# Moving the low halves of the weights to GpSimd and the high masks to VectorE in the attention of a hybrid decoder block

## Chip, cores and metric

The kernel runs on one core of one Trainium2 chip. The metric is the device time of one execution in microseconds; lower is better. A core has five engines that run their own instruction streams and wait for each other through semaphores: TensorE (PE in the profile; its weight loads stand apart as PEld), VectorE (DVE), ScalarE (ACT), GpSimd (POOL) and SyncE (SP, which here issues the DMAs).

## The reference

A decoder block over 512 tokens of width 2048, all in float32. After an RMS norm, one large projection feeds two branches: sliding-window attention (32 query heads, 4 key/value heads of width 64, window 128, a sink per head) and a gated delta rule (16 key heads, 32 value heads). Each branch is projected back, the two are merged by sigmoid gates, projected and added to the input, and a last norm follows. The attention, to which the change belongs, for each block of 128 queries and the 256 keys that it can see:

```python
s = jnp.einsum('bqhgd,bkhd->bhgqk', q_blk, k_blk).astype(jnp.float32) * scale
s = jnp.where((band & kv_ok[None, :])[None, None, None], s, -jnp.inf)
m = jnp.maximum(jnp.max(s, axis=-1, keepdims=True), sink)
p = jnp.exp(s - m)
p = p / (jnp.sum(p, axis=-1, keepdims=True) + jnp.exp(sink - m))
return jnp.einsum('bhgqk,bkhd->bqhgd', p.astype(v_blk.dtype), v_blk)
```

## The kernel before

**Precision by halves.** Every large product is made from three products of a shorter float format (fp32r): a value is split into a high half (`whi`, a cast by ACT) and a low half (`wlo`, the value minus its high half), and high x high, high x low and low x high are summed. For weights, `split` (L161) does this: one cast of 128x1024 (L162) and two subtractions of 128x512 (L165). The subtractions go to the engine that stands in `lo_eng[0]` at that time. Weight tiles come by DMA in half-tiles of 8 x 128 rows; `w32`, `whi` and `wlo` have three buffers each, so the cast for a half-tile waits until TensorE has done the high products of the third half-tile before it, and the subtractions until it has done that half-tile's low products.

**A projection** (`proj`, L183) is two half-tiles. `mm_half` (L171) does 16 matmuls with the high weights (L174, L176) and then 8 with the low weights (L179). After each matmul it calls `flow.tick()`.

**Order.** TensorE's instructions keep the order in which the program writes them. Other work is written as generators in `Flow`: each says after how many ticks it wants to go on, and its TensorE instructions are thereby placed between those of the projections. The order on DVE, ACT, POOL and SP is not written out; the framework that builds the program sorts each engine's instructions by when it reckons them ready and by their place in the program. At run time each engine takes its queue strictly in that order.

**Stages.** (1) norm and transposes, 0 to about 70 us; (2) key and query convolutions and their inverse matrices, to about 810; (3) the delta rule, to 1815, with `lo_eng[0] = pool` (L632); (4) the attention, 1815 to 2205, with `lo_eng[0] = dve` (L663); (5) the branch projections and merge, to 2726; (6) the output projection and last norm.

**The attention.** Four groups `g` of eight heads. While the projections of queries and of some gates run, `scores(g, b, ...)` (L703) handles the query block `b` = 0 to 3 in two halves of four heads (`i2`): per half, TensorE makes scores of four heads into two PSUM banks, `pa` and then `pb` (L717, L718); DVE adds the mask and takes the maximum (L722, it reads the bank) and folds the two key blocks into one by another maximum (L725; the window of 128 makes a key of the block before and one of this block exclude each other in every column); ACT takes the exponential and its sums (L733); DVE adds the sink's part (L734) and takes the reciprocal (L735); POOL normalizes (L736).

`weighted(g, b, scs)` (L747) follows some ticks later: per half, TensorE transposes the probabilities (L757), ACT casts them to the high half `pth` (L759) and DVE makes the low half `ptl` (L760). Both have an unmasked copy (index 0, for the block's own keys) and, if `b` is not 0, a masked one (index 1, for the difference to the block before): POOL masks the high half (L763), DVE the low half (L764), two instructions of 128x256 each per half. Then TensorE multiplies with the values (L774, into the banks `pc` and `tr`), ACT and DVE add the two parts (L776, L777), POOL multiplies with the gate (L778), and a DMA stores the result. `pth` and `ptl` have one buffer each.

Of the kernel before, what the change touches and what calls it, by code (L numbers as in the profile page):

```python
# [8 lines left out]
F32 = mybir.dt.float32  # L9
# [3 lines left out]
ALU = mybir.AluOpType  # L13
# [66 lines left out]
def hybrid_block(  # L80
# [21 lines left out]
    pe, dve, act, pool = nc.tensor, nc.vector, nc.scalar, nc.gpsimd  # L102
# [10 lines left out]
    def new_pool(stack, name, bufs, side="left"):  # L113
        return stack.enter_context(tc.tile_pool(name=name, bufs=bufs, side=side, reuse_waits="tile"))
# [4 lines left out]
    def bank(tag, bufs=1):  # L119
        return ps.tile([P, S], F32, name=tag, bufs=bufs)  # L120
# [31 lines left out]
    lo_eng = [dve]  # L152
# [507 lines left out]
                flow.drain()  # L660


    lo_eng[0] = dve  # L663
    actx = ctx.enter_context(ExitStack())
    pa = new_pool(actx, "pa_", 2)
    amask = pa.tile([P, 3 * P], F32, name="amask", bufs=1)
# [36 lines left out]
    def scores(g, b, qt, kd):  # L703
# [36 lines left out]
        def go():  # L740
            values_.add(weighted(g, b, scs))
            yield 0
# [4 lines left out]
    def weighted(g, b, scs):  # L747
        zs = pa.tile([P, 4, P], F32, name="za")
        nc.sync.dma_start(zs, za_d[4 * g:4 * g + 4, :, b * P:(b + 1) * P].rearrange("t p n -> p t n"))
        pth = pa.tile([P, 2, 2, 4, P], F32R, name="pth", bufs=1)  # L750
        ptl = pa.tile([P, 2, 2, 4, P], F32R, name="ptl", bufs=1)
        mb = before.unsqueeze(1).unsqueeze(1).broadcast_to([P, 2, 2, P])
        for i2, sc in enumerate(scs):
            tp = bank("tr", 2).rearrange("p (a j n) -> p a j n", a=2, j=2)
            for par in range(2):
                for j in range(2):
                    pe.transpose(tp[:, par, j, :], sc[:, 2 * j + par, :], ident)  # L757
            ph, pl = (pp[:, :, :, 2 * i2:2 * i2 + 2, :] for pp in (pth, ptl))
            act.copy(ph[:, :, 0], tp)  # L759
            dve.tensor_tensor(pl[:, :, 0], tp, ph[:, :, 0].bitcast(F32), ALU.subtract)  # L760
            if b:
                for a in range(2):
                    pool.tensor_tensor(ph[:, a, 1], ph[:, a, 0].bitcast(F32), mb[:, a], ALU.mult)  # L763
                    dve.tensor_tensor(pl[:, a, 1], pl[:, a, 0].bitcast(F32), mb[:, a], ALU.mult)  # L764
            yield 8
        done_b[0] += 1
        yield 4
        t = pa.tile([P, S], F32, name="at", bufs=1)
        oz = pa.tile([P, S], F32, name="gt").rearrange("p (i n) -> p i n", i=4)
        for par, r, r2 in ((0, H0, H1), (1, H1, H0)):  # L770
            op = bank("tr", 2) if par else bank("pc")
            todo = [(kind, n, pp) for kind in range(2 if b else 1) for n, pp in ((par, pth), (2 + par, ptl))]
            for i, (kind, n, pp) in enumerate(todo):
                pe.matmul(op, vpad[g % 2][kind][:, b - kind, n:n + 2, :].rearrange("p c d -> p (c d)"),  # L774
                          pp[:, par, kind].rearrange("p i n -> p (i n)"), start=i == 0, stop=i == len(todo) - 1)
            act.copy(t[r], op[r2])  # L776
            dve.tensor_tensor(t[r], t[r], op[r], ALU.add)  # L777
        pool.tensor_tensor(oz, t.rearrange("p (i n) -> p i n", i=4), zs, ALU.mult)  # L778
        nc.sync.dma_start(od_d[4 * g:4 * g + 4, :, b * P:(b + 1) * P].rearrange("t p n -> p t n"), oz)
        yield 6  # L780
# [39 lines left out]
    actx.close()  # L820


    op_ = new_pool(ctx, "op", 8)

    def branch(q, pl):
# [168 lines left out]
```

## Time and profile before

| | |
|---|---|
| median of 3 runs (range) | 2913.93 us (2913.84 to 2914.82) |
| the profiled execution: time, span | 2914.18 us, 2912.4 us |
| granted TensorE clock, mean | 0.997 |
| DMA moved, share of 16 engines by the large queue | 376.07 MB, 40.7% |
| attention, 1815 to 2205 us: ACT busy | 195.46 us |

The span is the time from the first to the last instruction in the trace; the time of the execution has a little more around it. A row of a group of instructions reads: line of the kernel, engine, operation, output<-inputs by the program's names, shape, count | busy time in us, mean duration of one in ns | idle time of the engine just before them and what ended it. A row of the timeline reads: start in us, duration in us, engine, line, operation, names, shape, count [idle time before it, and what ended it]; with a count over 1 the duration is that of several in a row. A row of waits reads: who waited for whom: total us, times, longest. A row of a stretch (A:B) has its length and then for each engine the busy us and the number of instructions (PE, PEld, DVE, ACT, POOL), the granted clock, the DMA share and GB/s. In the view of one line, a row has the shortest, median and longest duration in ns.

### The profile page before, as it was taken

What the parts mean: (1) busy time and instruction counts of PE and PEld (TensorE: products, weight loads), DVE (VectorE), ACT (ScalarE), POOL (GpSimd) and SP (SyncE); (2) the same over time, 40 slices, a digit from 0 to 9 for tenths busy, and PEclk for the clock granted to TensorE, in tenths of its full rate; (3) what the DMA queues carried; (4) which work ended last, traced back from release to release, by engine and by line L of the source; (5) the groups of instructions that cost most, each with busy time, mean ns of one, the idle gap of its engine ahead of it and who ended that gap; (6) DMA issues with size and microseconds to landing.
All of it is one profiled execution on the core that took longest, in us unless ns stands there. A gap on an engine that the chain in (4) does not pass through costs nothing.

```text
span 2912.4 us, 36773 instructions
## 1 busy us (share of the span) xinstructions
PE 2850.0 (98%) x13594; PEld 2370.9 (81%) x13594; DVE 1762.9 (61%) x3520; ACT 1028.6 (35%) x1645; POOL 555.8 (19%) x464
## 2 busy tenths in 40 slices
PE   7999999999999999999999999999999999999998
PEld 7778888888888888888878888877788888888887
DVE  6686667979825555555555554478884455455434
ACT  5532222232333343334333333355553222122222
POOL 2310000000033334333334333024230000000010
PEclk9999999999999999999999999999999999999999
DMA  3344444353553333333333322424237555554533
GB/s 132 115 123 142 135 136 151 125 207 116 174 153 100 103 110 103 105 98 116 98 109 109 104 89 94 133 87 113 91 109 225 172 174 163 156 163 147 181 100 103
DMA packets 184628, 376.07 MB, mean 129 GB/s; under 512 B 65505, under 2 KB 82273, under 8 KB 183041
## 3 DMA queue, kind: packets, MB, share of 16 engines
q1 hardware_dynamic: 184448, 373.72, 40.7%
q8 instruction: 108, 1.77, 0.3%
q14 instruction: 72, 0.58, 0.1%
HBM read 316.97 MB, written 54.59 MB: 128 GB/s over the span
## 4 chain that ended last, share of the span: by engine, by line
PE 88%; DVE 8%; ACT 2%; issue 1%; POOL 0%; DMA 0%; SPq 0%; ACTq 0%; DVEq 0%
PE acc L179 24%; PE acc L176 24%; PE acc L174 24%; PE pa L555 2%; PE pb L574 2%; PE fo L902 1%; PE fo L900 1%; PE fo L901 1%; PE acc L247 1%; PE tr L529 1%; DVE ptl L764 1%; DVE o L616 1%; DVE ro L197 1%; DVE wlo L165 1%; DVE ad L381 1%
## 5 line engine op out<-in xcount | busy, mean ns | idle before, releaser
L174 PE MATMUL acc<-hT_hi,whi 128*128 128x512 f32 x2592 | 1038.5, 401 | 0.0
L176 PE MATMUL acc<-hT_lo,whi 128*128 128x512 f32 x2592 | 1018.7, 393 | 0.0
L162 ACT CAST whi<-w 128x1024 fp32r<-128x1024 f32 x446 | 467.7, 1049 | 1166.5 <-PE acc L176 940.4
L179 PE MATMUL acc<-hT_hi,wlo 128*128 128x512 f32 x2592 | 685.1, 398 | 2.2 <-DVE wlo L165 2.2
L165 POOL TENSOR_TENSOR wlo<-w,whi 128x512 fp32r<-128x512 f32 x284 | 363.3, 1300 | 1231.8 <-PE acc L179 643.7
L165 DVE TENSOR_TENSOR wlo<-w,whi 128x512 fp32r<-128x512 f32 x608 | 424.0, 720 | 261.1 <-ACT whi L162 204.5
L176 PEld LDWEIGHTS acc<-hT_lo,whi 128*128 128x128 f32 x2592 | 488.6, 188 | 92.8
L174 PEld LDWEIGHTS acc<-hT_hi,whi 128*128 128x128 f32 x2592 | 488.3, 188 | 92.9
L179 PEld LDWEIGHTS acc<-hT_hi,wlo 128*128 128x128 f32 x2592 | 479.6, 188 | 98.1 <-DVE wlo L165 3.1
L176 PE MATMUL acc<-dl,whi 128*128 128x512 f32 x768 | 298.8, 389 | 0.0
L174 PE MATMUL acc<-dh,whi 128*128 128x512 f32 x768 | 298.8, 389 | 0.0
L179 PE MATMUL acc<-dh,wlo 128*128 128x512 f32 x768 | 189.7, 389 | 0.0
L297 DVE SCALAR_TENSOR_TENSOR cy<-acc,cw,cy 128x511 f32<-128x511 f32 (+2 forms) x192 | 142.8, 744 | 62.9 <-ACT cy L295 60.0
L863 DVE TENSOR_TENSOR gd<-acc,gl 128x512 f32<-128x512 f32 x80 | 55.3, 691 | 188.7 <-PE acc L179 188.7
L176 PEld LDWEIGHTS acc<-dl,whi 128*128 128x128 f32 x768 | 144.2, 188 | 30.0
L179 PEld LDWEIGHTS acc<-dh,wlo 128*128 128x128 f32 x768 | 144.1, 188 | 29.9
L174 PEld LDWEIGHTS acc<-dh,whi 128*128 128x128 f32 x768 | 144.1, 188 | 29.9
L562 DVE SCALAR_TENSOR_TENSOR rr<-pa,nbeG,vb 64x128 f32<-64x128 f32 x224 | 69.0, 348 | 143.2 <-PE pa L555 143.0
L920 POOL TENSOR_TENSOR y<-y,fw 128x512 f32<-128x512 f32 x12 | 18.9, 1605 | 658.7 <-ACT sqy L918 658.7
L566 ACT ACTIVATE xq<-pa,eGs 64x128 f32<-64x128 f32 x224 | 68.9, 356 | 170.1 <-DVE rr L562 167.6
L578 DVE TENSOR_TENSOR sv<-pb,eSuf 64x256 fp32r<-64x256 f32 x112 | 46.9, 418 | 116.7 <-PE pb L574 116.4
L467 DVE TENSOR_TENSOR m<-m,tm 128x62 f32<-128x62 f32 (+30 forms) x124 | 106.4, 858 | 2.8
(264 smaller groups left out, 3182.2 us busy)
## 6 DMA issues: line engine op xcount, KB each, us to landing
w<-w_in SPq DMA_DIRECT2D x326, 512.0 KB, 3.5
w<-w_dn SPq DMA_DIRECT2D x64, 512.0 KB, 3.5
gl<-ga_d SPq DMA_DIRECT2D x96, 256.0 KB, 2.6
w<-w_att SPq DMA_DIRECT2D x32, 512.0 KB, 3.8
w<-w_out SPq DMA_DIRECT2D x32, 512.0 KB, 3.5
of<-od_d SPq DMA_DIRECT2D x48, 256.0 KB, 3.9
kq_d<-slab SPq DMA_DIRECT2D x16, 512.0 KB, 2.8
ga_d<-gt SPq DMA_DIRECT2D x32, 256.0 KB, 3.8
```

What stands on the lines that cost most here:

```text
L162: act.copy(hi, w)
L165: lo_eng[0].tensor_sub(lo[:, r], w[:, r], hi[:, r].bitcast(F32))
L174: pe.matmul(acc, hi[:, k, :], rhi[k], start=first and k == 0, stop=False)
L176: pe.matmul(acc, hi[:, k, :], rlo[k], start=False, stop=False)
L179: pe.matmul(acc, lo[:, k, :], rhi[k], start=False, stop=last and k == n - 1)
L297: dve.scalar_tensor_tensor(y[:, sh:], acc[:, 0:S - sh], cw[:, t, 3 - sh:4 - sh], y[:, sh:], ALU.mult, ALU.add)
L467: dve.tensor_tensor(m[:, 0:jj, jj + 1:], m[:, 0:jj, jj + 1:], tm, ALU.add)
L555: pe.matmul(xp, slab[:, T, 2 * p:2 * p + 2, :].rearrange("d b i -> d (b i)"), s_cur, start=True, stop=True)
L562: dve.scalar_tensor_tensor(rr[rk, h, :], xp[rk, h, :], nbeG[rk, T, vh:vh + 1], vb[rk, T, h, :], ALU.mult, ALU.add)
L566: act.activation(xq[rq, h, :], xp[rq, h, :], AF.Copy, scale=eGs[rq, T, vh:vh + 1])
L574: pe.matmul(yp[:, h, :], tq[:, h * 4 + T, :], rr[:, h, :], start=True, stop=True)
L863: dve.tensor_tensor(gd, acc, gl, ALU.mult)
```

## The change

In the attention the low halves of the weights (L165) are made by GpSimd instead of VectorE, since `lo_eng[0]` is put back to `dve` only after the attention; and the masked copy of the high half of the probabilities (L763) is made by VectorE instead of GpSimd. What is computed stays the same.

```diff
@@ -660,7 +660,6 @@
                 flow.drain()
 
 
-    lo_eng[0] = dve
     actx = ctx.enter_context(ExitStack())
     pa = new_pool(actx, "pa_", 2)
     amask = pa.tile([P, 3 * P], F32, name="amask", bufs=1)
@@ -760,7 +759,7 @@
             dve.tensor_tensor(pl[:, :, 0], tp, ph[:, :, 0].bitcast(F32), ALU.subtract)
             if b:
                 for a in range(2):
-                    pool.tensor_tensor(ph[:, a, 1], ph[:, a, 0].bitcast(F32), mb[:, a], ALU.mult)
+                    dve.tensor_tensor(ph[:, a, 1], ph[:, a, 0].bitcast(F32), mb[:, a], ALU.mult)
                     dve.tensor_tensor(pl[:, a, 1], pl[:, a, 0].bitcast(F32), mb[:, a], ALU.mult)
             yield 8
         done_b[0] += 1
@@ -820,6 +819,7 @@
     actx.close()
 
 
+    lo_eng[0] = dve
     op_ = new_pool(ctx, "op", 8)
 
     def branch(q, pl):
```

## The prediction

> **What bounds the kernel now.** I read the page first: the share of each engine and the chain that ended last.
>
> ```profile
> PE 2850.0 (98%) x13594; PEld 2370.9 (81%) x13594; DVE 1762.9 (61%) x3520; ACT 1028.6 (35%) x1645; POOL 555.8 (19%) x464
> ...
> PE 88%; DVE 8%; ACT 2%; issue 1%; POOL 0%; DMA 0%; SPq 0%; ACTq 0%; DVEq 0%
> ```
>
> TensorE sets the time; whatever leaves it where it is costs and brings nothing. So the second view is who TensorE waits for in the attention (1815 to 2205 us), first for its matmuls, then for its weight loads, and the third is the busy time in that stretch.
>
> ```profile
> PE pc L774 <- DVE ptl L760: 4.0, 7, 0.7
> PE pb L717 <- DVE mx L722: 3.8, 4, 1.3
> PE pc L774 <- DVE ptl L764: 3.3, 7, 0.5
> ...
> PEld pc L774 <- DVE ptl L760: 7.4, 8, 1.2
> PEld pc L774 <- DVE ptl L764: 6.4, 7, 0.9
> PEld pb L717 <- DVE mx L722: 4.6, 4, 1.5
> ...
> 1815.00:2205.00 390.00, 378.91 (x1838) 312.55 (x1837) 279.56 (x729) 195.46 (x477) 100.99 (x101) 1.00 0.38 114
> ```
>
> Each wait row has the total, the number of waits and the longest. The matmuls lose 4.0 + 3.8 + 3.3 = **11.1 us**, all of it to VectorE (DVE); the weight loads, whose idle time also holds a part of the ordinary spacing, show 18.4 us. That is all there is to win: 0.4% to 0.6%. None of the waits is for `wlo`, the tile whose engine changes. They come in two places of each of the four groups of heads, which the timeline shows for group 1. I call the first **place A** (block 1 of the group). TensorE, then DVE, then POOL (GpSimd):
>
> ```profile
> 2009.31 0.39 PE L717 MATMUL pb<-kdh,q 128*128 128x256 f32 x1 [0.85 <-DVE mx L722]
> 2011.29 0.50 PE L774 MATMUL pc<-ptl,vpad 128*128 128x512 f32 x1 [0.54 <-DVE ptl L760]
> 2012.54 0.50 PE L774 MATMUL pc<-ptl,vpad 128*128 128x512 f32 x1 [0.51 <-DVE ptl L764]
> ...
> 2005.44 0.95 DVE L725 TENSOR_TENSOR sc<-sr 128x256 f32<-128x256 f32 x1
> 2006.32 2.13 DVE L764 TENSOR_TENSOR ptl<-ptl,amask 128x256 fp32r<-128x256 f32 x2
> ...
> 2010.07 0.43 DVE L725 TENSOR_TENSOR sc<-sr 128x256 f32<-128x256 f32 x1
> ...
> 2012.06 0.76 DVE L764 TENSOR_TENSOR ptl<-ptl,amask 128x256 fp32r<-128x256 f32 x2
> ...
> 2004.68 1.43 POOL L763 TENSOR_TENSOR pth<-pth,amask 128x256 fp32r<-128x256 f32 x2 [0.69 <-ACT pth L759]
> 2006.07 1.22 POOL L736 TENSOR_TENSOR sc<-sc,sm 128x512 f32<-128x512 f32 x1
> 2007.25 1.78 POOL L763 TENSOR_TENSOR pth<-pth,amask 128x256 fp32r<-128x256 f32 x2
> ```
>
> Two things are to be seen. DVE runs without a pause through A and has no `wlo` (L165) between its rows there: the work that the change takes from DVE is not in the burst that TensorE waits for. And the same pair of masks (L764) takes 2.13 us beside a busy POOL and 0.76 us beside an idle one, the maximum L725 0.95 against 0.43. **DVE and POOL hold each other up**: 1.37 + 0.52 = 1.89 us in this one burst. The spread of single operations says the same:
>
> ```profile
> L763 POOL TENSOR_TENSOR pth<-pth,amask x48: 728/904/1185, 1938.7 to 2178.8; 128x256 fp32r<-128x256 f32 x48
> ...
> L764 DVE TENSOR_TENSOR ptl<-ptl,amask x48: 410/814/1259, 1940.3 to 2179.7; 128x256 fp32r<-128x256 f32 x48
> ```
>
> [...]
>
> **The change part by part.** Both edits move work between exactly these two engines; no instruction is added to TensorE, ScalarE (ACT) or a DMA queue.
>
> ```profile
> L165 DVE TENSOR_TENSOR wlo<-w,whi 128x512 fp32r<-128x512 f32 x109 | 79.1, 752 | 53.6 <-ACT whi L162 41.4 <-PE acc L179 10.3 <-issue 0.9
> ...
> L763 POOL TENSOR_TENSOR pth<-pth,amask 128x256 fp32r<-128x256 f32 x48 | 40.7, 868 | 17.3 <-ACT pth L759 17.3
> ...
> L165 POOL TENSOR_TENSOR wlo<-w,whi x284: 1268/1289/2354, 814.7 to 1814.5; 128x512 fp32r<-128x512 f32 x142
> ...
> L179 PE MATMUL acc<-hT_hi,wlo 128*128 128x512 f32 x2592 | 685.1, 398 | 2.2 <-DVE wlo L165 2.2
> ```
>
> 1. *Low halves to POOL.* DVE loses 109 x 752 ns, of which 79.1 us are busy time. POOL gets as many at the 1289 ns that it takes in the stage before (the x284 row): 109 x 1.289 = 140 us.
> 2. *High masks to DVE.* POOL loses 40.7 us. DVE gets 48 masks of the same shape as L764; two of those in a row take 0.76 us and one takes 0.42, so one more costs 0.34: 16 us. Together DVE goes from 280 to about 217 us and POOL from 101 to about 200 us, not counting what they wait for each other.
> 3. *Is `wlo` late?* It has three buffers. POOL made 284 of them between 815 and 1815 us, and in the whole kernel TensorE's L179 waited 2.2 us for `wlo`, for one that DVE had made. In the attention the pair can now stand in POOL's queue behind L736 (which waits for DVE's sums) or L778 (for DVE's `at`), some microseconds; but with three buffers a pair made when one half-tile ends is needed only by the last third of the third half-tile after it. I cost it at nothing; without that cover each half-tile would wait the lateness itself.
> 4. *Is the softmax late?* L736, now also behind a pair of 2 x 1.29 = 2.6 us, ended at 2014.72 for a transpose at 2024.37: 9.6 us of cover, so nothing.
>
> ```profile
> 2013.68 1.04 POOL L736 TENSOR_TENSOR sc<-sc,sm 128x512 f32<-128x512 f32 x1 [4.64 <-DVE sm L735]
> ...
> 2024.37 0.38 PE L757 MATMUL tr<-ident,sc 128*128 128x128 f32 x2
> ```
>
> 5. *DMA.* The weight loads on SP's queue can start earlier, since POOL can read `w32` sooner than a crowded DVE; the DMA engines are 0.38 busy in the stretch (the window's row), so this costs nothing and brings nothing.
> 6. *Place A, four times.* TensorE waits for the end of DVE's unbroken burst, so its length is what counts. Out goes the present holding-up, -1.89 us. In come two high masks of the first half of the heads and one of the second ahead of the last wait: 3 x 0.34 = +1.02. And in comes the holding-up by what POOL does now, y. When does POOL run its pair? In the stage before, it starts as soon as TensorE has done the last L179 of a half-tile and so freed a buffer: the eight below end at 1112.05, POOL starts at 1112.19. In place A the last one of a half starts at 2004.16.
>
> ```profile
> 1109.96 2.09 PE L179 MATMUL acc<-hT_hi,wlo 128*128 128x512 f32 x8
> ...
> 1112.19 2.54 POOL L165 TENSOR_TENSOR wlo<-w,whi 128x512 fp32r<-128x512 f32 x2 [4.10 <-issue]
> ...
> 2004.16 0.40 PE L179 MATMUL acc<-hT_hi,wlo 128*128 128x512 f32 x1
> ```
>
> So the pair falls at about 2004.6, with L736 (1.04 us) behind it, and DVE's five operations with two SBUF inputs (L725 and now four masks) begin at 2005.44. Below, y is 0 if the program's order puts the pair elsewhere and L736 ahead of it. Above, all three POOL operations come between the five: 1.29 + 1.29 + 1.04 less the 0.9 that is over by 2005.44 makes 2.7. The nearest row is the 1.89 of today, at this place, with three POOL operations of 0.7 to 1.0 us alone; with longer ones I take 2.0. A: -1.89 + 1.02 + 2.0 = +1.13 us (from -0.87 to +1.83), four times **+4.5**.
> 7. *Place B, four times* (block 2 of each group). Here DVE does have `wlo` shortly before.
>
> ```profile
> 2024.54 0.66 DVE L760 TENSOR_TENSOR ptl<-tr,pth 128x512 fp32r<-128x512 f32 x1
> ...
> 2026.01 1.98 DVE L764 TENSOR_TENSOR ptl<-ptl,amask 128x256 fp32r<-128x256 f32 x2
> ...
> 2029.89 0.50 PE L774 MATMUL pc<-ptl,vpad 128*128 128x512 f32 x1 [0.51 <-DVE ptl L764]
> ...
> 2023.57 0.57 ACT L759 CAST pth<-tr 128x512 fp32r<-128x512 f32 x1
> ```
>
> L760 needs L759, which ends at 2024.14, and starts at 2024.54; with `wlo` gone it can start 0.4 earlier and no more: ACT is late next. The masks lose 1.98 - 0.76 = 1.22 of holding-up and gain 1.02 of masks. L736 still meets them; half of its 1.04 is my middle. B: -0.4 - 1.22 + 1.02 + 0.5 = -0.1 (from -0.6 to +1.1, where a 1.29 operation blocks in full and the 0.4 is lost), four times **-0.4**.
>
> The sum is +4.1 us. The profiled execution took 2914.18 us, a span of 2912.4 and 1.8 around it, 0.25 over the median of 2913.93. The forecast against the median is **2918.0 us**, +0.14%: within the 0.2% that a measurement of this kernel can tell from no change.
>
> **The rivals.** *The engines come apart (faster).* The pairs fall where DVE reads PSUM (L722, L760, L777, L809), y is near 0, and DVE, lighter by 63 us, comes earlier everywhere. For it: the two masks no longer hold each other up, and much of DVE's work here reads PSUM. Against it: A has no `wlo` in it, and POOL is twice as busy. A and B at their lower ends give 4 x 0.87 + 4 x 0.6 = 5.9 us; all the waits, 11.1 us. I put it between the two, at 2907.
>
> *The hold-up grows (slower).* The two engines alternate strictly, one POOL operation between two of DVE, in A and in B. For it: in the POOL rows of place A, L736 and L763 stretch from 1.04 to 1.22 and from 0.73 to 0.9 as DVE's do, so each takes its turn. [...] Against it: POOL would have to be busy at every one of the five. A and B at their upper ends: 4 x 1.83 + 4 x 1.1 = +11.7, so 2925.6. It decides from the point where A and B together cost over 5.8 / 4 = 1.45 us more than now in each group.
>
> *Nothing changes for TensorE.* The waits named in the first fences were never for `wlo`; if what leaves and what comes in A and B cancel, the time is 2914 to within a microsecond. The change then does on the engines what it says, and nothing for the end.
>
> [...]
>
> **How the numbers follow.** The forecast's case, partly held up, has 0.40, of which 0.06 lies beyond +0.2%; the faster rival 0.25; the slower 0.28; no change 0.07. So faster by over 0.2% has 0.25, within 0.2% 0.41, slower 0.34. The range: 2905 holds the faster rival to somewhat below its sum but not the 2902.8 of all waits gone; 2929 holds the slower rival's end and a few microseconds for waits at places that have none now, such as block 3, where the masks end just in time. What is left out on either side is 1 in 10.
>
> **What would show it.** In the profile after, the attention should have L165 on POOL x109 or so at 1.29 us and more, L763 on DVE x48, POOL busy near 200 us of the 390 and DVE near 220 to 250. Step 6 is right if the L725 and mask rows of place A still show durations near or over 1 us and TensorE's wait before `pb` L717 is longer than 0.85 us; it is wrong if these masks run in 0.34 us each. Step 7 is right if the waits before L774 in block 2 stay. Step 3 is wrong if TensorE waits for POOL's `wlo`, step 4 if it waits for L736. The prediction as a whole would be wrong by the order of the instructions: the order on DVE and POOL is worked out by the framework at build time, and with other loads it can put a mask or a pair elsewhere than I did.

## The result, and the profile after

The changed kernel takes **2937.49 us** (median; 2936.0 to 2940.49), the kernel before 2913.89 in the same comparison: 23.6 us more, a ratio of 1.0084 with an interval of 1.0068 to 1.01. It is slower, and by more than the range of the prediction held. The profiled execution took 2936.1 us, a span of 2934.3; before it was 2912.4. So 21.9 us of span are to be accounted for.

First the shares of the engines and of the chain that ended last, in the profile after:

```profile
PE 2856.9 (97%) x13594; PEld 2374.6 (81%) x13594; DVE 1737.3 (59%) x3472; ACT 1028.2 (35%) x1645; POOL 637.2 (22%) x512
...
PE 86%; DVE 9%; ACT 2%; issue 1%; DMA 0%; POOL 0%; SPq 0%; ACTq 0%; DVEq 0%
```

VectorE has less to do than before (1737.3 us against 1762.9), as meant, and yet has the larger share of the chain (9% against 8%). The stretches say where. The columns are those of the prediction's stretch; the attention now ends at about 2230 us instead of 2205:

```profile
1815.00:2230.00 415.00, 390.30 (x1842) 320.43 (x1841) 254.69 (x681) 195.52 (x476) 181.75 (x148) 0.98 0.36 109
2230.00:2934.00 704.00, 694.04 (x3101) 575.17 (x3099) 332.01 (x538) 178.68 (x222) 18.91 (x12) 1.00 0.49 155
```

These bounds are rounded; fixed points of TensorE's order tell it more closely. From the first transposes of the attention's values (L690 before, L689 after: 1855.93 and 1853.57 us) to the first low-weight matmul of the branch projections (2207.12 and 2229.02) it is 351.2 us before and 375.4 after, **24.3 more**; from there to the end 705.3 in both. The 2.4 us by which this exceeds the loss of span lie at the start: already at 43 us, where the kernels are the same, the profiled execution of the changed one was 2.2 us ahead. So the whole loss lies in the attention. In its stretch VectorE went from 279.56 to 254.69 us and GpSimd from 100.99 to 181.75. TensorE's busy time rose from 378.91 to 390.30 with four more matmuls in the stretch: it ran some of them more slowly, and the granted clock is 0.98 instead of 1.00. The waits of TensorE's matmuls in that stretch:

```profile
PE pc L773 <- DVE ptl L759: 11.0, 8, 3.0
PE pb L716 <- DVE mx L721: 8.9, 5, 2.1
PE pc L773 <- DVE ptl L763: 2.2, 3, 0.7
PE pc L773 <- DVE pth L762: 2.0, 3, 0.7
PE pc L773 <- ACT pth L758: 0.6, 1, 0.6
```

(Lines from L663 on have moved up by one: L773 is the old L774, L759 the old L760.) Together 24.7 us where there were 11.1: **13.6 us of the loss are longer waits, nearly all at the same two places**. Sorted by time, A has 11.8 us in the four groups (6.9 before), of which `pb` makes 8.2 (3.8 before); B has 11.9 (4.2 before); 0.9 lie elsewhere. None is for `wlo`. What VectorE's and GpSimd's operations of the change took in this stretch:

```profile
L165 POOL TENSOR_TENSOR wlo<-w,whi 128x512 fp32r<-128x512 f32 x96 | 125.5, 1326 | 105.4 <-PE acc L179 49.0 <-ACT whi L162 46.3 <-ACT osq L609 4.1
...
L763 DVE TENSOR_TENSOR ptl<-ptl,amask 128x256 fp32r<-128x256 f32 x48 | 30.8, 642 | 0.1
...
L762 DVE TENSOR_TENSOR pth<-pth,amask 128x256 fp32r<-128x256 f32 x48 | 28.0, 584 | 0.0
...
L165 DVE TENSOR_TENSOR wlo<-w,whi 128x512 fp32r<-128x512 f32 x14 | 10.8, 804 | 4.3 <-ACT whi L162 4.2
```

The masks average 584 and 642 ns, though a mask with nothing beside it takes 0.41 us. The timeline of place A in group 1 shows one such meeting (TensorE, VectorE, GpSimd):

```profile
2014.93 0.39 PE L716 MATMUL pb<-kdh,q 128*128 128x256 f32 x1 [2.06 <-DVE mx L721]
...
2009.95 0.83 DVE L762 TENSOR_TENSOR pth<-pth,amask 128x256 fp32r<-128x256 f32 x1
2010.70 1.51 DVE L763 TENSOR_TENSOR ptl<-ptl,amask 128x256 fp32r<-128x256 f32 x1
2012.14 1.25 DVE L762 TENSOR_TENSOR pth<-pth,amask 128x256 fp32r<-128x256 f32 x1
2013.32 0.41 DVE L763 TENSOR_TENSOR ptl<-ptl,amask 128x256 fp32r<-128x256 f32 x1
...
2009.20 2.73 POOL L165 TENSOR_TENSOR wlo<-w,whi 128x512 fp32r<-128x512 f32 x2 [0.27 <-ACT pth L758]
2011.89 1.22 POOL L735 TENSOR_TENSOR sc<-sc,sm 128x512 f32<-128x512 f32 x1
```

Three masks end one after another with GpSimd's three operations; only the fourth, with GpSimd idle, takes 0.41 us. The four last from 2009.95 to 2013.73 instead of 4 x 0.34 = 1.4 us, and TensorE waits 2.06 us for the bank `pb` where it waited 0.85. Place B of the same group (ScalarE, GpSimd, VectorE, TensorE):

```profile
2030.08 0.40 ACT L732 ACTIVATE sc<-sc,nm 128x128 f32<-128x128 f32 x1 [5.69 <-DVE es L728]
...
2031.73 1.03 ACT L162 CAST whi<-w 128x1024 fp32r<-128x1024 f32 x1
...
2032.48 1.04 POOL L735 TENSOR_TENSOR sc<-sc,sm 128x512 f32<-128x512 f32 x1 [2.51 <-DVE sm L734]
...
2033.48 2.72 POOL L165 TENSOR_TENSOR wlo<-w,whi 128x512 fp32r<-128x512 f32 x2
...
2033.89 1.16 DVE L762 TENSOR_TENSOR pth<-pth,amask 128x256 fp32r<-128x256 f32 x1
...
2034.97 1.51 DVE L763 TENSOR_TENSOR ptl<-ptl,amask 128x256 fp32r<-128x256 f32 x1
...
2036.41 0.41 DVE L762 TENSOR_TENSOR pth<-pth,amask 128x256 fp32r<-128x256 f32 x1
...
2038.70 0.49 PE L773 MATMUL pc<-ptl,vpad 128*128 128x512 f32 x1 [2.29 <-DVE ptl L759]
```

Here the pair of low halves falls on the masks too, and the rows tell how it got there. Its input is ScalarE's cast L162. That stands behind the exponentials (L732), the exponentials waited 5.69 us for VectorE's `es`, and on GpSimd the pair stands behind L735, which waits for VectorE's sums. So VectorE, by being late, lets the pair go just when its own masks begin.

The rest of the loss, 24.3 - 13.6 = 10.7 us, goes with the clock. These are two of the stretches in which the granted clock (the third figure from the right) was halved, and the sum over all six of them in the attention; before there was none:

```profile
2017.10:2020.50 3.40, 2.85 (x7) 1.94 (x7) 3.35 (x14) 1.62 (x7) 1.04 (x1) 0.50 0.00 0
2020.50:2023.90 3.40, 3.40 (x10) 2.63 (x9) 2.56 (x10) 2.77 (x9) 0.00 (x0) 0.50 0.00 0
...
sum 20.50, PE 19.94 PEld 15.33 DVE 12.31 ACT 8.68 POOL 1.04; mean PE 3.32 PEld 2.55 DVE 2.05 ACT 1.45 POOL 0.17
```

At half the clock 20.5 us can cost at most 10.2, which leaves 0.5 us open. In the timeline it shows as a run of eight matmuls of L179 that takes 3.21 us, where the prediction's row has 2.09:

```profile
2021.29 3.21 PE L179 MATMUL acc<-hT_hi,wlo 128*128 128x512 f32 x8
```

Each of the stretches begins within 2.4 us behind a wait at A or B: these two follow the 2.06 us of place A. The length of a single wait doesn't decide it, though: the stretch at 2191.1 follows one of 1.05 us, and the 2.03 to 2.06 us of place A in the other three groups are followed by none. The last section comes back to this.

### The profile page after: what moved, and what is told of

It is laid out like the page before. It is cut to its first block, busy times and chain, and to the rows that moved or that the text cites. A ratio compares the mean times of both kernels' runs of the same rounds, so it can differ in the third digit from the quotient of the medians.

```text
span 2934.3 us, 36834 instructions
## 1 busy us (share of the span) xinstructions
PE 2856.9 (97%) x13594; PEld 2374.6 (81%) x13594; DVE 1737.3 (59%) x3472; ACT 1028.2 (35%) x1645; POOL 637.2 (22%) x512
## 4 chain that ended last, share of the span: by engine, by line
PE 86%; DVE 9%; ACT 2%; issue 1%; DMA 0%; POOL 0%; SPq 0%; ACTq 0%; DVEq 0%
PE acc L179 24%; PE acc L176 23%; PE acc L174 23%; PE pa L555 2%; PE pb L574 2%; PE fo L900 1%; PE fo L902 1%; PE fo L901 1%; PE acc L247 1%; PE tr L529 1%; DVE o L616 1%; DVE ro L197 1%; DVE sr L721 1%; DVE pth L762 1%; DVE ad L381 1%
## 5 line engine op out<-in xcount | busy, mean ns | idle before, releaser
L162 ACT CAST whi<-w 128x1024 fp32r<-128x1024 f32 x446 | 467.6, 1049 | 1150.9 <-PE acc L176 937.3
L165 POOL TENSOR_TENSOR wlo<-w,whi 128x512 fp32r<-128x512 f32 x380 | 488.8, 1307 | 1337.5 <-PE acc L179 700.4
L179 PE MATMUL acc<-hT_hi,wlo 128*128 128x512 f32 x2592 | 689.0, 400 | 2.3 <-DVE wlo L165 2.3
L179 PEld LDWEIGHTS acc<-hT_hi,wlo 128*128 128x128 f32 x2592 | 483.2, 190 | 99.5 <-DVE wlo L165 3.1
L165 DVE TENSOR_TENSOR wlo<-w,whi 128x512 fp32r<-128x512 f32 x512 | 355.2, 716 | 212.1 <-ACT whi L162 167.8
L179 PE MATMUL acc<-dh,wlo 128*128 128x512 f32 x768 | 189.7, 389 | 0.0
L179 PEld LDWEIGHTS acc<-dh,wlo 128*128 128x128 f32 x768 | 144.2, 188 | 29.9
```

Source lines behind the costliest of these rows:

```text
L162: act.copy(hi, w)
L165: lo_eng[0].tensor_sub(lo[:, r], w[:, r], hi[:, r].bitcast(F32))
L179: pe.matmul(acc, lo[:, k, :], rhi[k], start=False, stop=last and k == n - 1)
```

## The experiments

Two theories stand against each other. **Hold-up:** VectorE's masks, which have two inputs in SBUF, and GpSimd's subtractions hold each other up where they meet, above all in A and B (in the profile after, the masks take at most 0.43 us with nothing of GpSimd beside them, up to 1.52 with it); TensorE waits longer there and then gets half clock. **Load:** it is the moved work itself, the masks on VectorE or the later and longer work on GpSimd (queue, late `wlo`), wherever it stands. The table has all runs; "waits" are those of TensorE's matmuls in the attention, "half" the number of stretches of 3.4 us at half clock there. Both are read from the one profiled execution of each kernel. The last column is a sum: the span before without its waits (2912.4 - 11.1 = 2901.3), plus the waits, plus 1.7 us for each such stretch (half of its 3.4 us).

| kernel | time, us | ratio to before | waits, us (longest) | half | span, us | sum, us |
|---|---|---|---|---|---|---|
| before | 2913.89 | | 11.1 (1.3) | 0 | 2912.4 | |
| after | 2937.49 | 1.0084 [1.0068, 1.01] | 24.7 (3.0) | 6 | 2934.3 | 2936.2 |
| low halves only | 2929.52 | 1.0055 [1.0038, 1.0072] | 19.7 (1.6) | 4 | 2928.0 | 2927.8 |
| masks only | 2908.87 | 0.9986 [0.9976, 0.9995] | 7.3 (0.7) | 0 | 2906.1 | 2908.6 |
| write only | 2913.93 | 1.0002 [0.9993, 1.0012] | 10.2 (1.0) | 0 | 2911.6 | 2911.5 |
| no high masks | 2924.30 | 1.0038 [1.0023, 1.0052] | 16.4 (1.6) | 4 | 2924.5 | 2924.5 |
| filled waits (+10.9) | 2931.18 | 1.0059 [1.0042, 1.0076] | 13.1 (2.1) | 3 | 2927.9 | 2930.4 |
| longer bursts, before | 2920.50 | 1.0023 [1.0014, 1.0032] | 12.4 (1.8) | 3 | 2919.3 | 2918.8 |
| no low halves | 2905.33 | 0.9971 [0.9959, 0.9983] | 5.2 (0.7) | 0 | 2903.4 | 2906.5 |
| later products | 2911.0 | 0.999 [0.9981, 1.0] | 8.5 (1.3) | 1 | 2911.2 | 2911.5 |
| high masks from PSUM | 2920.90 | 1.0021 [1.0012, 1.003] | 13.7 (2.7) | 3 | 2919.1 | 2920.1 |
| maxima first | 2925.29 | 1.0038 [1.0024, 1.0052] | 15.3 (3.1) | 5 | 2922.2 | 2925.1 |
| write only at B | 2926.37 | 1.0044 [1.0028, 1.0061] | 18.7 (2.1) | 3 | 2925.5 | 2925.1 |
| write only at A | 2929.24 | 1.0054 [1.0039, 1.0069] | 18.2 (2.9) | 5 | 2928.6 | 2928.0 |
| cast first | 2931.07 | 1.0064 [1.0048, 1.0081] | 20.4 (2.6) | 4 | 2927.1 | 2928.5 |
| cast and pair first | 2931.06 | 1.0059 [1.0044, 1.0074] | 19.2 (2.6) | 6 | 2930.4 | 2930.7 |

**Two terms account for every span within 3.1 us**: how long TensorE waits in the attention, and how many stretches at half clock follow. (A part of what is left is the start, where the profiled executions differ by up to 2.8 us ahead of the attention; for the attention alone, between the fixed points named above, the same sum holds within 1.5 us, and within 2.4 for "no low halves".) So the rows below ask where these two come from. One caution belongs ahead: an edit of the program also lets the framework sort the queues anew. In the trace, the order of VectorE, GpSimd and ScalarE in the attention stayed that of the changed kernel in "filled waits" and "write only at B" (apart from one or two instructions at the attention's start), so these price one thing alone. It nearly did in "write only" and "write only at A": at place A the normalization L735 stands between the four memsets there, where it stood behind the two subtractions, and in "write only" GpSimd's last few instructions are ordered otherwise. In the others the order moved with the edit.

**Each edit alone.** The changed kernel with the masks put back on GpSimd:

```diff
-                    dve.tensor_tensor(ph[:, a, 1], ph[:, a, 0].bitcast(F32), mb[:, a], ALU.mult)
+                    pool.tensor_tensor(ph[:, a, 1], ph[:, a, 0].bitcast(F32), mb[:, a], ALU.mult)
```

> Only the first edit: GpSimd makes the low halves in the attention, and keeps the masks of the high halves. Theory 'hold-up' (VectorE's operations with two SBUF inputs and GpSimd's operations shut each other out, and the 1.3 us low halves are what VectorE now waits for): no better than the changed kernel, since GpSimd has still more to do beside the masks of the low halves; 2925 to 2950 us. Rival 'load' (the 48 masks added to VectorE make its bursts longer, GpSimd does not matter): without the masks VectorE has 79 us less than before, so 2905 to 2915 us.

2929.52 us: moving the low halves costs 15.6 us by itself. The time lies in the range of "hold-up", but that theory also had this kernel no better than the changed one, and it is 8.0 us better. And the kernel before with the masks on VectorE (the same line, the other way, and `lo_eng[0] = dve` left at L663):

> Only the second edit: VectorE masks the high halves too, and keeps the low halves of the weights. Theory 'hold-up': the masks cost 0.34 us each and shut out only L736 and L778, so between a few us faster and a few slower than before: 2908 to 2922 us. Rival 'load': VectorE has 16 us more than before and no relief, so this is the slowest of all, over 2935 us.

2908.87 us: **faster than both kernels**, 5.0 us below the kernel before (by the interval of the ratio 1.5 to 7 us), so the masks are no costly load of their own on VectorE. The waits of TensorE in its attention:

```profile
PE pc L774 <- DVE ptl L760: 3.9, 7, 0.6
PE pc L774 <- DVE pth L763: 2.2, 3, 0.7
PE pb L717 <- DVE mx L722: 1.2, 4, 0.7
```

The bank `pb` is waited for 1.2 us instead of 3.8: with GpSimd out of the masks, the hold-up that the prediction priced at 1.89 us for place A is mostly gone: the 48 high masks take 512 ns in the mean, the 48 low ones 413 (725 before). The two edits don't add up: -5.0 and +15.6 make 10.6, and together they cost 23.6. A reason that fits, though no run isolates it: each mask that VectorE took is one more operation that GpSimd's subtractions can hold up.

**Write only.** The changed kernel, in which GpSimd writes zeros in place of the low halves of the attention's weights, in twice the instructions; these low halves are thus left out of the products:

```diff
-            lo_eng[0].tensor_sub(lo[:, r], w[:, r], hi[:, r].bitcast(F32))
+            if fill[0]:
+                for _ in range(2):
+                    pool.memset(lo[:, r].bitcast(F32), 0.0)
+            else:
+                lo_eng[0].tensor_sub(lo[:, r], w[:, r], hi[:, r].bitcast(F32))
```

> The changed kernel, but in the attention GpSimd fills each low half with zeros (four memsets per half-tile, about 2.4 us) in place of the two subtractions (2.6 us): it is as busy, at the same places of its queue, but reads nothing from SBUF. The low halves of the weights are left out there. Theory 'hold-up': the waits fall back to those of before or under them, masks and maxima at 0.35 us each, no low clock in the attention: 2900 to 2915 us. Rivals 'load' and 'queue' (what is late is what stands behind the low halves in GpSimd's queue): as the changed kernel, 2930 to 2942 us.

2913.93 us, 23.6 less than the changed kernel: the whole loss. VectorE's two groups of masks in its attention (from here on the experiments' lines are offset by a few):

```profile
L769 DVE TENSOR_TENSOR ptl<-ptl,amask 128x256 fp32r<-128x256 f32 x48 | 23.3, 485 | 0.1
L768 DVE TENSOR_TENSOR pth<-pth,amask 128x256 fp32r<-128x256 f32 x48 | 19.9, 415 | 0.0
```

and place B of group 1, GpSimd and then VectorE:

```profile
2024.23 1.93 POOL L168 MEMSET wlo<- 128x512 f32 x4
...
2024.68 0.41 DVE L768 TENSOR_TENSOR pth<-pth,amask 128x256 fp32r<-128x256 f32 x1
...
2025.02 0.42 DVE L769 TENSOR_TENSOR ptl<-ptl,amask 128x256 fp32r<-128x256 f32 x1
```

GpSimd is busy beside the same masks and they take 0.41 us, not 1.16 and 1.51. So it isn't GpSimd's being busy that holds VectorE up in these rows, but what it does: beside memsets, which only write, the masks keep their 0.41 us, and beside subtractions, which read `w` and `whi`, they do not. What VectorE does counts too: in the profile after, its subtraction L759, which reads one of its inputs from PSUM, takes at most 0.69 us, beside GpSimd's work as without it. The memsets need neither `w` nor `whi` and are shorter in sum (93.6 us against 125.5), so the time prices the reading and the length together; the 0.41 us of the masks beside a running memset does not depend on the length.

**Which pairs?** As above, but only the pairs that stand at place B (or A) are written, all others subtracted (for B three groups, for A four; for A the numbers are 20, 28, 38 and 46; `nth` counts the pairs of the attention):

```diff
+            if fill[0] and nth[0] - 1 in (22, 30, 40):
+                for _ in range(2):
+                    pool.memset(lo[:, r].bitcast(F32), 0.0)
```

> The changed kernel, in which the pairs of low halves that stand at place B (block 2 of groups 0 to 2: the pairs with the numbers 22, 30 and 40 of the attention) are only written by GpSimd (memsets), and all others are subtracted as before. It leaves out the low halves of those three half-tiles of weights. Theory (the pair that stands behind the normalization in GpSimd's queue falls on the masks, makes them 1.2 to 1.5 us instead of 0.41, and TensorE waits there and then runs a stretch at half clock): the waits of place B fall from some 4.0 us to some 1.5 in three groups, 7.5 us, and up to three stretches at half clock, at most 5 us, go with them: 2924 to 2931. Rival (it is not these pairs, but the whole load of 96 subtractions beside VectorE's work): 2936 to 2940, with the waits of B where they were.

> The same for place A: the pairs with the numbers 20, 28, 38 and 46 (block 1 of the four groups) are only written; the low halves of those four half-tiles of weights are left out. Theory: the waits of place A fall from some 3.9 us to some 2.3 in four groups, 6.4 us, and up to two stretches at half clock, at most 3.5 us, go with them: 2926 to 2932. Rival (as above): 2936 to 2940.

2926.37 and 2929.24 us: 11.1 and 8.3 us less than the changed kernel, both as the theory had it. TensorE's longest groups of waits, first with B's pairs written, then with A's:

```profile
PE pb L723 <- DVE mx L728: 8.8, 5, 2.1
PE pc L780 <- DVE ptl L766: 5.1, 8, 1.1
```

```profile
PE pc L780 <- DVE ptl L766: 11.2, 8, 2.9
PE pb L723 <- DVE mx L728: 2.8, 5, 0.7
```

Each takes away the waits of its own place (11.0 to 5.1 for `ptl`; 8.9 to 2.8 for `pb`) and leaves the other's as they were. With B's pairs written, place B of group 1 looks like this (GpSimd, then VectorE):

```profile
2031.37 1.93 POOL L169 MEMSET wlo<- 128x512 f32 x4
...
2031.80 0.42 DVE L769 TENSOR_TENSOR pth<-pth,amask 128x256 fp32r<-128x256 f32 x1
2032.14 0.42 DVE L770 TENSOR_TENSOR ptl<-ptl,amask 128x256 fp32r<-128x256 f32 x1
```

The memsets run at the pair's place beside the same masks, GpSimd has nothing else to do for 5.75 us behind them, and TensorE's wait there falls from 2.29 to 0.44 us. So it is neither the sum of GpSimd's work nor what stands behind the pair in its queue. **Seven of the 48 pairs, each place priced by itself and the two added, make 19.4 of the 23.6 us.** The run at B, where the order stayed, settles the cause for its place; at A the normalization moved with the edit, so the 8.3 us hold that too.

**Is the half clock the waits' doing?** The changed kernel with matmuls put where TensorE would wait (48 in all, 48 x 0.227 = 10.9 us by the spacing of its matmuls; in the profile after, eleven of 128x512 begin between 1915.65 and 1917.94, 0.229 apart):

```diff
+            for _ in range({1: 3, 2: 9}.get(b, 0) if par == 0 else 0):
+                pe.matmul(op, vpad[g % 2][0][:, b, 0:2, :].rearrange("p c d -> p (c d)"),
+                          pth[:, 0, 0].rearrange("p i n -> p (i n)"), start=True, stop=True)
```

> The changed kernel, with TensorE given 3 extra matmuls in block 1 and 9 in block 2 of each group, in front of the value products (their results are overwritten by the first real one): 48 matmuls of 0.227 us, 10.9 us of work, set where TensorE stands and waits for VectorE. Theory 'clock' (the six 3.4 us stretches of half clock in the attention of the changed kernel come from TensorE standing idle for 2 us and more, and cost some 7 to 9 us): fewer of these stretches, and 2925 to 2934 us although TensorE does more. Rival (the clock falls for another reason): the stretches stay and the time is 2937 to 2945 us.

2931.18 us: 6.3 us faster than the changed kernel with 10.9 us more to do. Its waits are 11.6 us shorter, which the added matmuls eat up; the gain comes with the stretches at half clock, three instead of six. It did not take all of them: place A's 2.1 us remain. The opposite, longer bursts of VectorE in the kernel before, with GpSimd's work untouched:

```diff
             dve.tensor_tensor(pl[:, :, 0], tp, ph[:, :, 0].bitcast(F32), ALU.subtract)
+            if b in (1, 2) and i2 == 0:
+                for _ in range(3):
+                    dve.tensor_tensor(pl[:, :, 0], tp, ph[:, :, 0].bitcast(F32), ALU.subtract)
```

> The kernel before with VectorE's L760 done four times in place of once for the first half of blocks 1 and 2 of each group: 3 x 0.6 = 1.8 us more in each of eight bursts, read from PSUM, with GpSimd's work as it was. Theory 'a burst is waited for as long as it is': TensorE's waits grow by up to 8 x 1.8 = 14 us; theory 'clock': half-clock stretches appear in the attention without any change on GpSimd and add some us; 2924 to 2938 us. Rival (only the two engines' shutting out costs time): under 2918 us and no half clock.

2920.50 us misses both expectations: only 1.3 us of waits were added, and the order moved with the edit. But three stretches at half clock came, with none of GpSimd's work changed. In the table, kernels whose longest wait is at most 1.0 us have no such stretch, those with 1.3 none or one, those with 1.6 and more three to six. That the stretches come from waits is thus an inference over 16 kernels, and not the result of one clean run; the last section has a closer look.

**Less work.** The changed kernel without the 48 high masks, and the changed kernel without the low halves:

```diff
-                    dve.tensor_tensor(ph[:, a, 1], ph[:, a, 0].bitcast(F32), mb[:, a], ALU.mult)
...
-                          pp[:, par, kind].rearrange("p i n -> p (i n)"), start=i == 0, stop=i == len(todo) - 1)
+                          pp[:, par, kind if pp is ptl else 0].rearrange("p i n -> p (i n)"), start=i == 0, stop=i == len(todo) - 1)
```

> The changed kernel without the 48 masks of the high halves on any engine: TensorE reads the unmasked copy in their place, so the high halves of the probabilities stay unmasked for the block before. Theory 'hold-up': half of the operations that can be shut out are gone, but the low halves still meet the other masks: 2912 to 2926 us. Rival 'load': the price of the added masks is all, so at or under the kernel before: 2900 to 2912 us.

```diff
         act.copy(hi, w)
+        if fill[0]:
+            return hi, hi
```

> The changed kernel without any subtraction for the low halves in the attention: TensorE takes the high half in place of the low one. Theory 'the low halves on VectorE were never in the burst': VectorE is free of them and GpSimd too, yet the time is only that of the write-only run or a little less, 2906 to 2914 us. Rival 'VectorE's load counts': well under the kernel with the masks alone (2908.9), at 2898 to 2904 us.

2924.30: even without the high masks anywhere, the low halves on GpSimd cost 10.4 us over before. 2905.33: without any low halves it is 8.6 us under before, between the two expectations and nearer to that of "never in the burst". It is also 8.6 us under "write only", which still has 5.0 us more waits. The order of the two differs, so whether that is the memsets' doing or the order's stays open.

**Can the pairs be put elsewhere?** The cast goes ahead of the exponentials in ScalarE's queue, and in the second kernel also the pair ahead of the second normalization in GpSimd's:

```diff
+            with tc.high_priority():
+                act.copy(hi, w)
...
+                with tc.high_priority():
+                    lo_eng[0].tensor_sub(lo[:, r], w[:, r], hi[:, r].bitcast(F32))
```

> The changed kernel, all of its work done, with ScalarE's cast of the weights (the input of the pair of low halves) put ahead of the exponentials in its queue. TensorE's order is the same, VectorE's nearly. Theory (the pair falls on the masks of place B because the cast waits in the queue behind exponentials that wait for VectorE): the cast comes some 2.7 us earlier there, but some pairs now straddle a normalization on GpSimd, so about half of what e11 gained: 2926 to 2934, with place A as it was (2.0 us before the scores of each group). Rival (the cast's place doesn't decide where the pair falls, or exponentials held up behind the cast cost as much): 2935 or more.

> As e13, and the pair of low halves also goes ahead of the second normalization in GpSimd's queue. Theory: the pair is over before the masks of place B begin, these take some 0.41 us each, and TensorE's waits at place B fall from some 3.5 us in a group to some 1.5, with up to three stretches at half clock gone: 2924 to 2931, as when those pairs were only written (2926.37). Rival: 2935 or more; or a new wait, for the normalization or the low half itself, shows in TensorE's waits.

2931.07 and 2931.06 us, 6.4 less than the changed kernel; the first as expected, the second just past the end of its range and no better than the first. Place B in the second kernel, group 1:

```profile
2030.65 1.03 ACT L165 CAST whi<-w 128x1024 fp32r<-128x1024 f32 x1
...
2031.82 2.56 POOL L172 TENSOR_TENSOR wlo<-w,whi 128x512 fp32r<-128x512 f32 x2 [1.69 <-ACT whi L165]
...
2034.06 0.60 DVE L772 TENSOR_TENSOR pth<-pth,amask 128x256 fp32r<-128x256 f32 x1
...
2034.34 1.22 POOL L745 TENSOR_TENSOR sc<-sc,sm 128x512 f32<-128x512 f32 x1
2034.58 1.26 DVE L773 TENSOR_TENSOR ptl<-ptl,amask 128x256 fp32r<-128x256 f32 x1
```

The cast comes 1.1 us earlier and the pair 1.7 us: it now meets the end of one mask only, 0.60 us, but the normalization that it overtook meets the next, 1.26 us. TensorE's waits for `ptl` fell from 11.0 to 6.2 us. The order of the queues does decide where the pair falls, and so a part of the loss; the place it leaves is taken by another reading operation.

**Towards a better kernel.** Three variants of "masks only" tried to win the rest: value products 12 ticks later (`yield 16` instead of `yield 4` in `weighted`), the high masks taken from PSUM instead of SBUF, and the maxima L722 with high priority.

> The kernel with the masks alone on VectorE, and the value products set 16 matmuls behind the last transposes in place of 4 (12 x 0.227 = 2.7 us later in TensorE's order), so that the bursts of VectorE end before TensorE comes to them. If TensorE's waits for the masks and low halves of the probabilities were all that is left there, 2 to 8 us faster than the masks alone: 2901 to 2907 us. If the wait only moves to the banks of the scores, the same, 2907 to 2911 us.

> The masks alone on VectorE, but the masked high half is made straight from the transposes in PSUM (transpose times mask, rounded on writing) in place of from the high half in SBUF: one SBUF input, so that GpSimd cannot shut it out, and no wait for ScalarE's cast. Theory 'hold-up': the 48 masks no longer show 1 us beside GpSimd, each takes some 0.45 us, and the time is at or up to 5 us under that of the masks alone (2908.9): 2903 to 2909 us. Rival (what is left there is the length of VectorE's bursts): the longer reading from PSUM makes it 2909 to 2914 us.

```diff
+            if b:
+                for a in range(2):
+                    dve.tensor_tensor(ph[:, a, 1], tp[:, a], mb[:, a], ALU.mult)
             dve.tensor_tensor(pl[:, :, 0], tp, ph[:, :, 0].bitcast(F32), ALU.subtract)
...
-                    dve.tensor_tensor(ph[:, a, 1], ph[:, a, 0].bitcast(F32), mb[:, a], ALU.mult)
```

> The masks alone on VectorE, with the maxima that free the banks of the scores (L722) ordered ahead of other VectorE work that is ready. If the order within VectorE's bursts is what TensorE still waits for, the waits for the banks (1.2 us) go and the time is 2904 to 2909 us; if the bursts' length counts, the waits move to the value products and the time is 2908 to 2914 us.

2911.0, 2920.90 and 2925.29 us: none beats "masks only". In the first, within its second expectation, the waits only changed places (8.5 us in sum); its interval overlaps that of "masks only". The other two miss both of theirs. In the second the masks with one input in PSUM do run at 412 ns in the mean and 425 at most, but the edit writes them ahead of the low half, for which TensorE then waits 13.3 us. In the third the waits for the score banks are all but gone, and 11.3 us of waits for `ptl` come instead: it does the same work as "masks only" in another order, and that alone costs 16.4 us. The fastest version is the change's second edit alone, 2908.87 us.

## Why the prediction was wrong

It had the mechanism and the two places; of the two sizes it had one, in part by luck, and one cost it left out. Against its own steps:

- **Step 1** (low halves to GpSimd): right in kind. 96 subtractions moved, not 109: the stretch of the count held 13 of the next stage, which stay on VectorE (the x14 row). They take 1326 ns for the 1289 assumed, and GpSimd came to 181.75 us instead of 200.
- **Step 2**: VectorE came to 254.69 us, in a stretch that is 25 us longer and holds 10.8 us of the next stage's low halves, where 217 was worked out without hold-up; the 16 us for 48 masks became 28.0, and the 48 low masks came to 30.8 (32.9 before), where they take 23.3 in "write only".
- **Steps 3, 4 and 5**: right as far as they went. TensorE never waits for `wlo` in the attention, nor is L735 named as the one it waits for. But step 3 asked only whether a late pair makes `wlo` late. It named the queue behind L736 and costed it at nothing; it didn't ask what the lateness does to the pair's place.
- **Step 6** (place A): right. The waits of A went from 6.9 to 11.8 us, +4.9 in four groups (+4.4 of them for `pb`), where +4.5 was forecast. That the size fits so well is partly luck: the hold-up y was 2.4 us in group 1 (3.78 less 4 x 0.34), where 2.0 was taken, and the third of the masks added, priced at 0.34, made the last wait of a group longer by some 0.2 at most. The pair fell about where it was put: it began 5.7 us ahead of the matmul of `pb` (2009.20 and 2014.93), where 4.7 was worked out (2004.6 and 2009.31).
- **Step 7** (place B) is **the step that failed**: forecast -0.4 us, measured +7.8 us of waits (from 4.2 to 11.9). It let only half of an L736 meet the masks, 0.5 us, and no pair of low halves. In the new order the whole pair falls on them in three groups; in group 1 the first two masks take 1.16 and 1.51 us. With these three pairs only written, 11.1 us go. It also counted four groups, though in the fourth TensorE waited only 0.5 us at B before. Its upper end, +1.1, took an operation of 1.29 us to block a mask in full, and no run shows that: the longest mask at B in group 1, 1.51 us, was 1.10 over its 0.41 beside subtractions of 1.36.
- **A term that was missing:** the clock. The sum took TensorE's matmuls as before; six stretches at half clock cost some 10 us, more than twice the forecast's whole sum.

Of the rivals, "the hold-up grows" came nearest in kind: strict alternation, one operation of GpSimd to one of VectorE, is what the timeline of place A shows. Its price (11.7 us) is near the 13.6 us of waits; it lacked the clock. "The engines come apart" is out: at A and B the pairs fell beside the masks and not beside work of VectorE that reads PSUM. (That such work goes free of GpSimd the profile before shows: there L722 took at most 0.49 us and L760 0.69, beside GpSimd's work (57 and 24 times) as without it.) The prediction's last sentence, that the order is worked out anew by the framework, named the risk, but its range ends at 2929 us and leaves little room for it.

## What to carry to other kernels

Where two engines hold each other's instructions up, as VectorE and GpSimd do here (masks of 0.41 us took 1.16 and 1.51), moving work from the busy one to the idle one is priced by which instructions then meet, not by the busy time that is saved: look for each moved operation's releaser, ask where it would run if the queue ahead of it is late, and count what it meets there in full. Work that goes to VectorE and takes reading operations off GpSimd can be a gain (5.0 us here), and work that goes the other way a loss (15.6 us), though the second frees the busier engine. And where a change makes the waits of a TensorE-bound kernel longer, look at its granted clock in the stretch right behind them and add that to the price: here 20.5 us at half clock came to some 10 of the 24.3 us lost in the attention.

## What the runs showed of the hardware

TensorE's clock was halved in stretches of 3.4 us; the longest wait in the attention of any of these kernels was 3.1 us. The stretch of the changed kernel just ahead of the two shown above, with the 2.06 us of place A in it:

```profile
2013.60:2017.10 3.50, 1.63 (x8) 1.15 (x8) 3.40 (x12) 1.39 (x5) 0.00 (x0) 1.00 0.32 128
```

TensorE was busy for 1.63 of these 3.50 us, and then ran at half clock for 6.8.

The traces of the changed kernel and of the kernel before have more on this. In the attention of the changed kernel there are five records of half clock: four of 3413 ns and one of 6827. They begin 15, 7, 24 and 20 times 3.413 us apart. Cut into intervals of that length, counted from the first of these records, the attention has five intervals at full clock with half clock right behind them; TensorE's matmul rows are busy in them for 1.12, 1.59, 1.51, 0.83 and 1.81 of the 3.41 us. The least busy of the intervals that are followed by full clock have 1.64, 1.93, 1.79, 1.94 and 2.13. So the four below 1.6 us were followed by half clock, of the five from 1.64 to 1.94 us only that of 1.81, and of those above none. The 2.03 us of place A in group 0 were split between the intervals with 1.64 and 1.93 us busy, and nothing followed. In the kernel before, cut in the same way from its last record ahead of the attention, the least busy interval of the attention has 2.2 us, and none is followed by half clock. These are two traces; a limit that holds elsewhere they don't show.

The clock also differs between executions of one kernel: the four of the changed kernel have a mean granted clock of 0.991 to 0.994, and the one with 0.991 took longest, 2940.49 us. Whether they differ in the number of stretches in the attention, the one profiled execution doesn't show.
